# A conv and attention layer in fp32: written order for the convolution's output stage, the norm's rows sooner, and h in x's place

## The chip, the cores and the metric

The kernel runs on one core of a Trainium2 chip. The metric is the device time of one execution in microseconds. The kernel before was timed three times: 1240.5, 1238.94 and 1238.16, a median of 1238.94 us.

Six instruction streams work side by side and meet only at semaphores: PE (TensorE, matrix products), DVE (VectorE), ACT (ScalarE, which also evaluates functions from tables), POOL (GpSimd), SP (SyncE, which issues most of the transfers) and the DMA engines.

## The reference, cut to what matters

One decoder layer over 1024 positions and 1024 channels, with a convolution branch and an attention branch.

```python
mod = c @ w_ada + b_ada
shift, scale, gate = split(mod, 3)
h = _rmsnorm(x, norm_g) * (1.0 + scale) + shift
glu_a, glu_b, z_conv, q, k, v, z_att, g_conv, g_att = split(h @ w_in)

u = glu_a * sigmoid(glu_b)
u = causal_depthwise_conv(u, conv_w, 31 taps) + conv_b
u = silu(_layernorm(u, conv_ln_g, conv_ln_b))
y_conv = (u * silu(z_conv)) @ w_conv_out

att = dilated_window_attention(rope(q, positions), rope(k, positions), v)   # three groups of heads
y_att = (att * silu(z_att)) @ w_att_out
merged = sigmoid(g_conv) * y_conv + sigmoid(g_att) * y_att
return _rmsnorm(x + gate * (merged @ w_o), final_g)
```

The change touches four things in it: how `h` is kept, the layer norm over channels of `u`, the product with `w_conv_out`, and the tables of sines and cosines from `positions`.

## The kernel before

**Layout.** Activations lie with channels in the 128 partitions, eight tiles of 128x1024 for 1024 channels (tile index `kt` or `ct`). A product in fp32 is made from three products of split values: `hh` and `hl` are the high and low part of `h`, `whi` and `wlo` those of a weight, `uh` and `ul` those of the convolution's result `u`. A helper `mm3` (L72 to L75) issues high times high, high times low and low times high, each a matmul of 512 columns. ACT makes high parts by a copy, DVE or POOL makes low parts by a subtraction. A weight arrives as a raw tile `wraw` (128x1024, three of them in turn, loaded by SP at L62).

**Start stage.** `scaled(kt)` (L351) multiplies x by the row of reciprocal norms into `xr` on DVE, and ACT writes it twice with scale and shift (L356): to `hh`, and in full precision to a tile `h`, of which there are two in turn (tag `h32`). SP stores `h` to the scratch `hscr` (L357), and DVE subtracts to get `hl` (L387). The PE loop around L387 takes one tile a turn, 18 matmuls each: three weights, two halves, three products. `shift(kt)` is a weighted sum on DVE over a row of `w_ada` (L169). Later the scratch is read back as `traw` (L512, L515) for the Strassen products, whose sums and differences DVE makes (L525 to L528, L538).

**The hand-written order.** From there to the norm an order by steps holds. A list `groups` has one entry for a group of twelve matmuls. At step n the loop issues what is due: early work, then the group of that step, then evictions and high parts on ACT, low parts on POOL, DVE work, and last the loads; `at(step, rank, fn)` books such work. A `Form` books a weight half's high part three steps ahead of its group and the low part two steps ahead; its tiles `whi`, `wlo` are handed out in turn from three pairs of 128x1024, in halves. A `Raw` books a load. Generators in the list `behind` are DVE work without a due step (the convolution's taps, the norm): `pump` takes pieces from them as a step's budget allows.

**The norm.** When the last convolution is summed, `norm_mean` (L785) makes the row of means on PE (`pm`), `norm_squares` subtracts it (L795) and sums squares on ACT and DVE (L798 to L803). `sums` books the column sums on PE (L128) two steps on; `scales` makes the reciprocal root a step later: ACT's Sqrt with its table load (L112), small operations on DVE (L113 to L117), and the row `lrow` on PE (L818). `norm_apply` (from L828) goes over the eight tiles `vt` of u: times `lrow` on DVE (L834), silu in two halves into PSUM (L837), times `sz` = silu(z_conv) on DVE (L848), high part `uh` on ACT (L851), low part `ul` on POOL (L852). Meanwhile PE runs the last products of the values; ACT copies their results out as `gs` (L633) and SP stores them to `vscr` (L634).

**The output stage.** Behind the loop stand, in program order: the tables from `positions` as one block on DVE (L969 to L988) with two sines on ACT (L983); then the product with `w_conv_out`. Units `d` = 0 to 7 are output tiles of 128 channels. Units 0 and 1 run side by side over the eight tiles of u, 96 matmuls; the other units run one after the other with `project`. Weights come through `weights` (L57 high on ACT, L58 low on DVE, 1024 wide). A unit's result is multiplied by the gate `sgc` on DVE (L1001) and stored (L1002); `modulation` makes a column of `gate_c` from a row of `w_ada` and the broadcast `cb` of c (L169). Attention follows.

## Time and profile before

| quantity | before |
|---|---|
| median of three runs | 1238.94 us (1238.16 to 1240.5) |
| profiled execution | 1237.25 us |
| its span, first to last instruction | 1235.5 us |
| mean granted TensorE clock | 0.986 |
| moved by DMA | 194.49 MB, mean 157 GB/s |

Busy shares and waits follow with the prediction. A timeline row reads: start in us, duration in us, engine, source line, operation, output <- inputs, shape, count, and in brackets the idle time ahead of it with what released it. A wait row reads: the waiting engine, line and tile <- the releaser, then the total, the number of times and the longest. A window row has its stretch, its length, and for each of PE, PE's weight loads, DVE, ACT and POOL the busy time with the number of instructions, then the granted clock, the share of DMA engines busy and GB/s. A DMA row gives the source line's tiles, the count, the size and the median us from issue to landing.

### The profile page before, as it was taken

To read this page: it belongs to the slowest core of one execution; us is meant where nothing else is said; L and a number is where in the kernel's file an instruction comes from. 1 tells how busy PE (TensorE), PEld (TensorE's weight loads), DVE (VectorE), ACT (ScalarE), POOL (GpSimd) and SP (SyncE) were. 2 spreads that over 40 slices of the span, in tenths; PEclk is the share of its full clock that TensorE was granted. 3 is DMA by queue.
4 is the path that set the end of the run, shared out by engine and by line. 5 is a ranking of instruction groups with operands and counts; after the bars stand their busy time and mean duration, and the time that the engine had idled before them with its cause. 6 is when DMAs were issued, how large, how long until landed. Compare 5 with 4: busy or idle time off the path is not lost.

```text
span 1235.5 us, 17342 instructions
## 1 busy us (share of the span) xinstructions
PE 1195.6 (97%) x6042; PEld 1000.4 (81%) x6042; DVE 910.8 (74%) x1500; ACT 585.8 (47%) x1205; POOL 404.1 (33%) x304
## 2 busy tenths in 40 slices
PE   9989999999999999588999999999999999999997
PEld 7777888888888888466888888888888888888886
DVE  7869999999999998684325657777786762559444
ACT  5645334545445445631015666666666655346111
POOL 0003868787787774430031111111111012200000
PEclk9989999999999999888999999999999999999999
DMA  9574333213324247717825555666665564668231
GB/s 361 194 260 169 120 103 120 97 65 103 113 84 136 71 152 289 276 48 251 195 82 150 137 137 144 160 188 144 159 193 144 141 181 132 207 236 298 86 102 68
DMA packets 100189, 194.49 MB, mean 157 GB/s; under 512 B 29635, under 2 KB 43267, under 8 KB 100102
## 3 DMA queue, kind: packets, MB, share of 16 engines
q1 hardware_dynamic: 83424, 186.77, 49.1%
q10 hardware_dynamic: 16678, 6.61, 1.9%
q8 instruction: 48, 0.79, 0.3%
q14 instruction: 39, 0.32, 0.1%
HBM read 122.25 MB, written 39.62 MB: 131 GB/s over the span
## 4 chain that ended last, share of the span: by engine, by line
PE 81%; DVE 11%; ACT 3%; DMA 3%; issue 1%; POOL 0%; SPq 0%; DVEq 0%; ACTq 0%
PE d L73 20%; PE d L75 20%; PE d L74 20%; DVE acc L566 5%; PE o L1308 4%; PE d L624 4%; PE s L1271 3%; PE t L1287 3%; PE d L1601 2%; PE d L1599 2%; PE d L1600 2%; DMA x<-in_xT 1%; DMA wraw<-in_w_v 1%; DVE wa L169 1%; ACT d L837 1%
## 5 line engine op out<-in xcount | busy, mean ns | idle before, releaser
L566 DVE SCALAR_TENSOR_TENSOR acc<-u,cw,acc 128x1024 f32<-128x1024 f32 x232 | 298.8, 1288 | 6.6
L74 PE MATMUL d<-hl,whi 128*128 128x512 f32 x752 | 294.5, 392 | 4.1 <-DVE hl L387 4.1
L73 PE MATMUL d<-hh,whi 128*128 128x512 f32 x752 | 295.8, 393 | 1.2 <-ACT gs L897 0.7
L75 PE MATMUL d<-hh,wlo 128*128 128x512 f32 x752 | 294.4, 391 | 0.5 <-POOL wlo L458 0.5
L58 POOL TENSOR_TENSOR wlo<-wraw,whi 128x512 fp32r<-128x512 f32 (+1 forms) x56 | 81.7, 1476 | 458.5 <-ACT whi L57 433.4
L458 POOL TENSOR_TENSOR wlo<-wraw,whi 128x512 fp32r<-128x512 f32 x114 | 151.7, 1338 | 183.6 <-ACT whi L455 173.3
L75 PEld LDWEIGHTS d<-hh,wlo 128*128 128x128 f32 x752 | 141.8, 189 | 31.3 <-POOL wlo L458 0.9
L74 PEld LDWEIGHTS d<-hl,whi 128*128 128x128 f32 x752 | 141.8, 189 | 30.5 <-DVE hl L387 4.5
L73 PEld LDWEIGHTS d<-hh,whi 128*128 128x128 f32 x752 | 141.8, 189 | 28.5 <-ACT gs L897 1.2
L1280 ACT ACTIVATE sb<-sb,stats 128x128 f32<-128x128 f32 (+1 forms) x192 | 84.8, 443 | 31.7 <-DVE stats L1276 31.4
L1276 DVE CUSTOM_DVE_ANT_0 sb<-s,mask 128x128 f32<-128x128 f32 (+1 forms) x192 | 59.7, 349 | 52.1 <-PE s L1271 50.8
L455 ACT ACTIVATE whi<-wraw 128x512 fp32r<-128x512 f32 x114 | 69.6, 625 | 42.8 <-POOL wraw L728 22.5
L57 ACT ACTIVATE whi<-wraw 128x512 fp32r<-128x512 f32 (+1 forms) x71 | 48.9, 718 | 78.6 <-PE d L74 66.5
L73 PE MATMUL d<-uh,whi 128*128 128x512 f32 x128 | 52.9, 413 | 22.3 <-DVE vt L848 12.7
L1287 PE MATMUL t<-ident,sb 128*128 128x128 f32 x280 | 73.7, 276 | 0.1
L1308 PE MATMUL o<-ph,vt 128*64 128x128 f32 (+1 forms) x432 | 65.9, 253 | 0.0
L1102 ACT ACTIVATE ph<-t 128x384 fp32r<-128x384 f32 (+2 forms) x96 | 45.7, 476 | 38.9 <-PE t L1287 25.8
L1105 DVE TENSOR_TENSOR pl<-t,ph 128x384 fp32r<-128x384 f32 (+2 forms) x96 | 52.0, 542 | 11.4 <-ACT ph L1102 10.8
L1271 PE MATMUL s<-k,ql 128*128 128x128 f32 (+1 forms) x192 | 55.0, 292 | 0.0
L1308 PE MATMUL o<-pl,vt 128*64 128x128 f32 (+1 forms) x216 | 52.8, 261 | 0.0
L74 PE MATMUL d<-ul,whi 128*128 128x512 f32 x128 | 51.9, 405 | 0.0
L1601 PE MATMUL d<-oh,hl 128*128 128x512 f32 (+1 forms) x136 | 51.2, 376 | 0.0
(295 smaller groups left out, 2631.5 us busy)
## 6 DMA issues: line engine op xcount, KB each, us to landing
wraw<-in_w_t SPq DMA_DIRECT2D x67, 512.0 KB, 4.1
k<-kqp SPq DMA_DIRECT2D x96, 128.0 KB, 2.3
q<-kqp SPq DMA_DIRECT2D x96, 128.0 KB, 2.3
wraw<-in_w_v SPq DMA_DIRECT2D x19, 512.0 KB, 4.4
wa<-in_w_ada SPq DMA_DIRECT2D x16, 512.0 KB, 4.8
ql<-kqp SPq DMA_DIRECT2D x48, 128.0 KB, 2.3
wg<-wscr SPq DMA_DIRECT2D x48, 128.0 KB, 3.2
hscr<-h SPq DMA_DIRECT2D x8, 512.0 KB, 2.6
```

Of the source, the lines that this page charges most:

```text
L58: (lo_eng or nc.vector).tensor_sub(lo, raw, hi.bitcast(F32))
L73: nc.tensor.matmul(ps, lh, rh, start=start, stop=False, skip_group_check=again)
L74: nc.tensor.matmul(ps, lh, rl, start=False, stop=False, skip_group_check=again)
L75: nc.tensor.matmul(ps, ll, rh, start=False, stop=stop, skip_group_check=again)
L455: nc.scalar.activation(self.hi, src(), AF.Copy)
L458: nc.gpsimd.tensor_sub(self.lo, src(), self.hi.bitcast(F32))
L566: nc.vector.scalar_tensor_tensor(acc, u[:, k:k + S], cw[:, ct, k:k + 1], acc, op0=mult, op1=add)
L1271: products.append((w, lambda c=c, w=w, l=x[:, ts_], r=k[:, ks], i=i: nc.tensor.matmul(ps[:, c:c + w], l, r, start=i == 0, stop=i == 1)))
L1280: nc.scalar.activation(sb[:, c:c + w], sb[:, c:c + w], AF.Exp, bias=stats[:, t, h, 1:2], scale=-1.0, accum_out=stats[:, t, h, 0:1])
L1287: yield from ((lambda c=c: nc.tensor.transpose(ps[:, c:c + P], sb[:, c:c + P], ident)) for c in range(0, o, P))
L1308: nc.tensor.matmul(out_, l, r, **kw))
L1601: nc.tensor.matmul(ps, hl[:, k, c], rh, start=False, stop=k == KT - 1)
```

## The change

1. `scaled` writes the full-precision `h` back into x's own tile; the two `h32` tiles go (one is left for another use).
2. Scratch space for half tiles becomes whole slots `n3`, `s1`, `sd0`, `sd1`, handed out by halves; the second set of `traw` is loaded two steps later and handled in whole tiles, its high and low parts one step later.
3. The norm's mean is due one step sooner, its column sums one step sooner after the squares, and its scales in the same step as the sums. `norm_apply` holds two PSUM banks for the silus instead of two for each tile, and issues the products of a tile ahead of the next tile's multiply by `lrow`.
4. The tables become a generator `tables` behind the norm.
5. The output stage is part of the list of groups: `first_outputs` makes eight groups, one for each tile of u, with units 0 and 1 side by side; `output` makes four groups for each further unit. Their weights come through `Raw` and `Form`; `Gated` loads the gate and the row of `w_ada` (into a raw tile) two steps ahead of its unit and does the sums in place. `cb` is loaded into the slot of the last `vt` tile.

```diff
-            return st.tile([P, S], F32, name="vs", tag="h32", bufs=2)
+            return st.tile([P, S], F32, name="vs", tag="h32", bufs=1)
...
         def scaled(kt):
             xr = st.tile([P, S], F32, name="xr", tag="xr", bufs=2)
-            h32 = h_of[kt] = st.tile([P, S], F32, name="h32", tag="h32", bufs=2)
+            h32 = h_of[kt] = x_t[kt]
             nc.vector.tensor_mul(xr, x_t[kt], rrow)
             for dst in (hh[:, kt], h32):
                 nc.scalar.activation(dst, xr, AF.Identity, bias=scol[:, kt:kt + 1], scale=gcol[:, kt:kt + 1])
...
-    for x in ("n2", "n3", "n4", "h3", "l3"):
+    for x in ("n2", "n4", "h3", "l3"):
         slot(x, "t")
-    piece("t", "s1", 2), piece("t", "side", 3), piece("t", "gs", 4), piece("t", "pad", 1)
-    for n in range(16):
-        slot(f"t{n}", "t")
+    piece("t", "gs", 4)
+    for x in ("n3", "s1", "sd0", "sd1", *(f"t{n}" for n in range(16))):
+        slot(x, "t")
...
-        return [[t[k] if type(t) is list else t[:, k] for t in tiles] for k in range(2)]
+            tag = ({1: "t1", 3: "t3", 2: "t5", 4: "t8"}, {1: "sd0", 3: "sd1", 2: "s1", 4: "n3"})[c][i]
+            raw = t_raw[i, c] = slot(tag, "traw").rearrange("p (k s) -> p k s", k=2)
+            nc.sync.dma_start(raw, hscr[k0 + 2 * c:k0 + 2 * c + 2, :, wide(half)].rearrange("k p s -> p k s"))
...
-            at(now[0] + 3, EARLY, norm_mean)
+            at(now[0] + 2, EARLY, norm_mean)
...
         def s1():
-            box["s1"] = piece("s1", "s1", 2)
+            box["s1"] = half_piece(("s1",))
...
         def copy(key, src, scale=1.0, sbuf=True):
             def fn():
-                box[key] = piece("side", "side", 3) if sbuf else bank()
+                box[key] = half_piece(("sd0", "sd1")) if sbuf else bank()
                 nc.scalar.activation(box[key], box[src], AF.Copy, scale=scale)
...
         def sums():
             pc = bank()[:, 0:8]
             col_sums(pc, tot2)
-            at(now[0] + 1, POST_, lambda: scales(pc))
-        at(now[0] + 2, EARLY, sums)
+            at(now[0], POST_, lambda: scales(pc))
+        at(now[0] + 1, EARLY, sums)
...
     def norm_apply(lrow):
         for ct in range(4):
             sz_load(ct)
-        sg = {}
+        sg = [bank() for _ in range(2)]
 
         def scaled_(ct):
             nc.vector.tensor_mul(vt[ct], vt[ct], lrow)
-            sg[ct] = [bank() for _ in range(2)]
             for half in range(2):
-                nc.scalar.activation(sg[ct][half], vt[ct][:, wide(half)], AF.Silu, scale=cvec[:, 1, ct:ct + 1],
+                nc.scalar.activation(sg[half], vt[ct][:, wide(half)], AF.Silu, scale=cvec[:, 1, ct:ct + 1],
                                      bias=cvec[:, 2, ct:ct + 1])
 
         scaled_(0)
         yield TAP
         for ct in range(KT):
+            for half in range(2):
+                s = wide(half)
+                nc.vector.tensor_mul(vt[ct][:, s], sg[half], sz_t[ct][:, s])
+            yield 2 * POST
+            hi, lo = slot(f"t{8 + ct}", f"uh{ct}", F32R), slot(f"t{ct - 1}" if ct else "n2", f"ul{ct}", F32R)
+            nc.scalar.activation(hi, vt[ct], AF.Copy)
             if ct + 1 < KT:
                 scaled_(ct + 1)
                 yield TAP
-            for half in range(2):
-                s = wide(half)
-                nc.vector.tensor_mul(vt[ct][:, s], sg[ct][half], sz_t[ct][:, s])
-            yield 2 * POST
-            hi, lo = slot(f"t{8 + ct}", f"uh{ct}", F32R), slot(f"t{ct - 1}" if ct else "n2", f"ul{ct}", F32R)
-            nc.scalar.activation(hi, vt[ct], AF.Copy)
             nc.gpsimd.tensor_sub(lo, vt[ct], hi.bitcast(F32))
             ch[ct], cl[ct] = hi, lo
             if ct + 4 < KT:
                 sz_load(ct + 4)
+        u_ctx.close()
+        tabs.append(c_ctx.enter_context(sbuf_pool("tabs", side="right")))
+        behind.append(tables())
...
+    def tables():
+        ctab, stab = (tabs[0].tile([P, S], F32, name=x) for x in ("ctab", "stab"))
+        tabs.extend((ctab, stab))
+        posi = pb.tile([P, S], I32, name="posi", tag="s1")
+        nc.sync.dma_start(posi, a["positions"].to_broadcast([P, S]))
+        yield GROUP
+        n_ = slot("sd0", "n_")
+        nc.vector.tensor_copy(n_, posi)
+        nc.vector.tensor_scalar(stab, n_, fr[:, 0:1], None, op0=mult)
...
+        for c in (C1, C2, C3):
+            nc.vector.scalar_tensor_tensor(stab, n_, -c, stab, op0=mult, op1=add)
+            yield TAP
...
+        def wrapped_sin(tab, n_):
+            nc.vector.tensor_scalar(n_, tab, PI_IN, -TWO_PI, op0=ALU.is_gt, op1=mult)
+            nc.vector.tensor_add(tab, tab, n_)
+            yield POST + TAP
...
+            yield POST
+            at(now[0] + 1, EVICT, lambda: nc.scalar.activation(tab, n_, AF.Sin))
+
+        nc.vector.tensor_scalar(ctab, stab, TWO_PI / 4, None, op0=add)
+        yield POST
+        yield from wrapped_sin(ctab, n_)
+        yield from wrapped_sin(stab, slot("sd1", "m_"))
+        at(now[0] + 2, POST_, lambda: nc.vector.tensor_scalar(stab, stab, fr[:, 1:2], None, op0=mult))
+
+    cb_of = []
+
+    def cb_load():
+        cb_of.append(slot("t7", "cb"))
+        nc.sync.dma_start(cb_of[0], a["c"].to_broadcast([P, D]))
+
...
+    class Gated:
+
+
+        def __init__(self, step, d):
+            self.d = d
+            at(step - 2, LOAD, self.load)
+
+        def load(self):
+            self.sg = slot(f"n{3 + self.d % 2}", "sgc")
+            nc.sync.dma_start(self.sg, gcscr[self.d])
+            self.wa = load_raw(a["w_ada"][2 * KT + self.d])
+
+        def out(self, half, ps):
+            y = piece("gs", "gs", 4)
+            nc.vector.tensor_mul(y, ps, self.sg[:, wide(half)])
+            spend(POST)
+            nc.sync.dma_start(cscr[self.d][:, wide(half)], y)
+            if half:
+                modulation(2 * KT + self.d, gate_c[:, self.d:self.d + 1], self.wa, self.wa, cb_of[0])
+                spend(TAP)
+
+    def u_block(kh, half):
+        s = wide(half)
+        return lambda k: (ch[4 * kh + k][:, s], cl[4 * kh + k][:, s])
+
+    def first_outputs(step):
+        raws = [Raw(step - 7 + d, a["w_co"][d]) for d in range(2)]
+        forms = {(d, kh): Form(step - 3 + 2 * kh + d, raws[d].half(kh)) for kh in range(2) for d in range(2)}
+        out = [Gated(step + 6 + d, d) for d in range(2)]
+        ps = {}
+
+        def group(k):
+            def fn():
+                for d in range(2):
+                    f = forms[d, k // 4]
+                    c = slice(k % 4 * P, k % 4 * P + P)
+                    for half in range(2):
+                        if k == 0:
+                            ps[d, half] = bank()
+                        mm3(ps[d, half], f.hi[:, c], f.lo[:, c], ch[k][:, wide(half)], cl[k][:, wide(half)],
+                            k == 0, k == KT - 1)
+                if k == KT - 1:
+                    for d in range(2):
+                        for half in range(2):
+                            at(now[0], POST_, lambda d=d, half=half: out[d].out(half, ps[d, half]))
+            return fn
+        return [group(k) for k in range(KT)]
...
+    def output(step, d):
+        raw = Raw(step - 6, a["w_co"][d])
+        forms = [Form(step + 2 * i, raw.half(i)) for i in range(2)]
+        out = Gated(step, d)
...
+        def group(i, half):
+            def fn():
+                if i == 0:
+                    ps[half] = bank()
+                block(ps[half], forms[i], u_block(i, half), i == 0, i == 1)
+                if i:
+                    at(now[0], POST_, lambda: out.out(half, ps[half]))
+            return fn
+        return [group(i, half) for i in range(2) for half in range(2)]
...
+    at(len(groups), LOAD, cb_load)
+    take(first_outputs(len(groups)))
+    for d in range(2, KT):
+        take(output(len(groups), d))
 
     at(-1, HIGH, t_first)
-    at(-1, LOAD, lambda: t_loads(1))
-    at(1, POST_, t_second)
+    at(1, LOAD, lambda: t_loads(1))
...
-    stab = tabs.tile([P, S], F32, name="stab")
-    posi = pb.tile([P, S], I32, name="posi", tag="h3")
-    nc.sync.dma_start(posi, a["positions"].to_broadcast([P, S]))
...
-    cb = slot("h3", "cb")
-
-    def co_load(d):
-        sg_ = slot(f"n{3 + d % 2}", "sgc")
-        nc.sync.dma_start(sg_, gcscr[d])
-        return weights(a["w_co"][d]), sg_
...
-    def gated(d, sg_, wa):
-        def consume(half, s, ps):
-            y = pb.tile([P, 512], F32, name="gs", tag="gs", bufs=4)
-            nc.vector.tensor_mul(y, ps, sg_[:, s])
-            nc.sync.dma_start(cscr[d][:, s], y)
-            if not half:
-                modulation(2 * KT + d, gate_c[:, d:d + 1], wa, slot("l3", "jk"), cb)
-        return consume
...
-    nc.sync.dma_start(cb, a["c"].to_broadcast([P, D]))
-    pair = [co_load(d) for d in range(2)]
-    ps = [bank() for _ in range(4)]
-    for k in range(KT):
-        c = slice(k * P, (k + 1) * P)
-        for i, ((hi, lo), _) in enumerate(pair):
-            for half in range(2):
-                s = wide(half)
-                mm3(ps[2 * i + half], hi[:, c], lo[:, c], ch[k][:, s], cl[k][:, s], k == 0, k == KT - 1)
...
-    ahead = co_load(2)
-    for d in range(2, KT):
-        w, sg_ = ahead
-        if d + 1 < KT:
-            ahead = co_load(d + 1)
-        project(w, gated(d, sg_, wada(d)), KT, lambda k, s: ch[k][:, s], lambda k, s: cl[k][:, s])
+
+    ctab, stab = tabs[1:]
```

The first place is ACT around the norm's reciprocal root. `vt_…` and `uh_…` with a number are single tiles of u, `d` is a PSUM bank, `ACT_TABLE_LOAD` loads a function table. Before:

```order
L455 ACTIVATE whi<-wraw 128x512 x3
L57 ACTIVATE whi<-wraw 128x1024
L112 ACT_TABLE_LOAD
L112 ACTIVATE ltmp<-lcols 128x8
L837 ACT_TABLE_LOAD
L837 ACTIVATE d<-vt_3768,cvec 128x512 x2
L837 ACTIVATE d<-vt_3770,cvec 128x512 x2
L851 ACTIVATE uh_4099<-vt_3768 128x1024
L57 ACTIVATE whi<-wraw 128x1024
```

And in the changed kernel:

```order
L455 ACTIVATE whi<-wraw 128x512 x3
L112 ACT_TABLE_LOAD
L112 ACTIVATE ltmp<-lcols 128x8
L455 ACTIVATE whi<-wraw 128x512 x2
L826 ACT_TABLE_LOAD
L826 ACTIVATE d<-vt_3697,cvec 128x512 x2
L837 ACTIVATE uh_3993<-vt_3697 128x1024
L826 ACTIVATE d<-vt_3699,cvec 128x512 x2
L455 ACTIVATE whi<-wraw 128x512 x2
L837 ACTIVATE uh_4022<-vt_3699 128x1024
```

The last of the three `whi` ahead of the Sqrt is now a half of the first output weight, two more halves stand between Sqrt and Silu, and each `uh` stands ahead of the next tile's silus instead of behind them.

The second place is SP's queue from the output weights on. Before:

```order
L62 DMA wraw<-in_w_ada 128x1024 x2
L967 DMA posi<-in_positions 128x1024
L1010 DMA cb<-in_c 128x1024
L826 DMA sz<-szscr_100 128x1024
L634 DMA vscr<-gs 128x512 x4
L826 DMA sz<-szscr_101 128x1024
L826 DMA sz<-szscr_102 128x1024
L826 DMA sz<-szscr_103 128x1024
L62 DMA wraw<-in_w_co 128x1024
L995 DMA sgc<-gcscr 128x1024 x2
L62 DMA wraw<-in_w_co 128x1024
```

And in the changed kernel:

```order
L615 DMA vscr<-gs 128x512 x4
L892 DMA cb<-in_c 128x1024
L856 DMA posi<-in_positions 128x1024
L62 DMA wraw<-in_w_co 128x1024
L903 DMA sgc<-gcscr 128x1024
L62 DMA wraw<-in_w_ada 128x1024
L903 DMA sgc<-gcscr 128x1024
L62 DMA wraw<-in_w_ada 128x1024
L903 DMA sgc<-gcscr 128x1024
L62 DMA wraw<-in_w_ada 128x1024
L62 DMA wraw<-in_w_co 128x1024
```

`cb` and `posi` moved behind the values' stores, the third `w_co` stands right behind them, and three rows of `w_ada` stand between it and the fourth.

The third place is DVE behind the norm's last product, in the changed kernel; before, all rows of the tables stood in one block there, ahead of the first `gs`:

```order
L868 SCALAR_TENSOR_TENSOR stab<-n__4203,stab 128x1024 x3
L882 TENSOR_SCALAR ctab<-stab 128x1024
L872 TENSOR_SCALAR n__4203<-ctab 128x1024
L873 TENSOR_TENSOR ctab<-ctab,n__4203 128x1024
L908 TENSOR_TENSOR gs<-d,sgc 128x512 x2
L169 ISA wraw,gate_c<-wraw,cb 128x1024
L169 ISA gate_c 128x1
L172 TENSOR_TENSOR gate_c<-gate_c,bada 128x1
L908 TENSOR_TENSOR gs<-d,sgc 128x512 x2
L169 ISA wraw,gate_c<-wraw,cb 128x1024
```

The gating and sums of units 0 and 1 now stand between pieces of the tables; nine more rows of the tables follow behind them and among those of units 2 and 3.

More of the change, by code (lines that the diff above doesn't have):

```diff
@@ L958, in layer @@
             step += 1
-    u_ctx.close()
-    c_ctx = ExitStack()
-    tabs = c_ctx.enter_context(sbuf_pool("tabs", side="right"))
-    ctab = tabs.tile([P, S], F32, name="ctab")
-    stab = tabs.tile([P, S], F32, name="stab")
-    posi = pb.tile([P, S], I32, name="posi", tag="h3")
-    nc.sync.dma_start(posi, a["positions"].to_broadcast([P, S]))
-    n_ = slot("l3", "n_")
-    nc.vector.tensor_copy(n_, posi)
-    nc.vector.tensor_scalar(stab, n_, fr[:, 0:1], None, op0=mult)
-    nc.vector.tensor_scalar(n_, stab, 1.0 / TWO_PI, None, op0=mult)
```

80 lines of the change are left out of this document (30 added, 50 removed).

## The prediction

> **What bounds the kernel now.** I read the page's busy shares and slices first, then the waits of TensorE (PE), then windows and timelines around the long ones.
>
> ```profile
> PE 1195.6 (97%) x6042; PEld 1000.4 (81%) x6042; DVE 910.8 (74%) x1500; ACT 585.8 (47%) x1205; POOL 404.1 (33%) x304
> PE   9989999999999999588999999999999999999997
> PEclk9989999999999999888999999999999999999999
> PE d L73 <- DVE vt L848: 12.7, 1, 12.7
> PE d L73 <- ACT whi L57: 9.6, 2, 5.4
> PE d L74 <- DVE hl L387: 4.1, 1, 4.1
> PE d L143 <- ACT rrow L144: 1.4, 1, 1.4
> PE d L73 <- DVE u L689: 0.5, 1, 0.5
> 130.00:475.00 345.00, 344.53 (x1519) 284.71 (x1518) 329.90 (x288) 153.08 (x260) 266.23 (x205) 1.00 0.34 112
> 512.50:566.00 53.50, 31.22 (x112) 24.38 (x112) 45.41 (x52) 23.51 (x30) 19.69 (x8) 0.78 0.41 142
> ```
>
> PE is busy 97% of the span, so the time is PE's work plus what PE waits. The wait rows (total, times, longest) name two places: 4.1 us for `hl` early on, and 12.7 + 9.6 = 22.3 us around the convolution's output stage, slices 17 to 19. From 130 to 475 us PE is busy 344.53 of 345 us (first number of the row): nothing the change does there can be worth much. A second loss hides inside busy time: in 512.5 to 566 the clock column says 0.78.
>
> ```profile
> 67.61 0.39 PE L73 MATMUL d<-hh,whi 128*128 128x512 f32 x1
> 72.06 0.80 PE L74 MATMUL d<-hl,whi 128*128 128x512 f32 x1 [4.07 <-DVE hl L387]
> ...
> 74.79 0.63 PE L74 MATMUL d<-hl,whi 128*128 128x512 f32 x1
> 75.22 0.63 PE L75 MATMUL d<-hh,wlo 128*128 128x512 f32 x1
> ...
> 555.53 0.80 PE L73 MATMUL d<-uh,whi 128*128 128x512 f32 x1 [5.36 <-ACT whi L57]
> ...
> 561.82 0.80 PE L73 MATMUL d<-uh,whi 128*128 128x512 f32 x1 [4.22 <-ACT whi L57]
> ```
>
> A warm matmul of 512 columns costs 344.53/1519 = 0.227 us (a group of 12 costs 2.72). After the 4.07 us wait the spacing is 0.43 us (74.79 to 75.22): 0.2 us more each. This holds from 72.06 to 77.3, some 13 matmuls, so 2.6 us in all are paid after such a wait; the rows at 555.53 and 561.82, with their 0.80 us, begin the same. Behind the 1.4 us wait (`rrow`) stand no slow matmuls.
>
> So the region 512.5 to 566 loses 53.5 − 112 × 0.227 = **28.1 us**: 22.3 of waits, 5.8 of slow clock. The early place loses 4.07 + 2.6 = **6.7 us**.
>
> **Part A, h in x's place.** ACT's write of `h` waited 5.69 us for the store of an older `h` from one of two tiles; behind it stood `hl`, behind that PE:
>
> ```profile
> 66.60 2.89 DMA hscr<-h
> 69.51 1.24 ACT L356 ACTIVATE h<-xr,scol,gcol 128x1024 f32<-128x1024 f32 x1 [5.69 <-DMA hscr<-h]
> 74.40 1.23 DVE L387 TENSOR_TENSOR hl<-h,hh 128x1024 fp32r<-128x1024 f32 x1
> 78.02 1.22 DVE L387 TENSOR_TENSOR hl<-h,hh 128x1024 fp32r<-128x1024 f32 x1
> ```
>
> With eight x tiles as targets no write waits for a store. `h` of the third tile then runs right behind its `hh` near 63.8 us, `hl` follows on DVE by about 66.3, and PE needs it at 67.8. What is late next is DVE, one `hl` each 78.02 − 74.40 = 3.62 us; PE spends 18 × 0.227 = 4.09 us on a tile, so DVE keeps ahead. Of the 6.7 us I keep **6.0**: the stage behind hangs on the last stores to `hscr`, the raw loads and DVE's chain to `u`, for which PE already waits 0.5 us; it moves up by the stall of 5.69 at most. If the stage follows only in part, 2 remain; at best 6.7.
>
> The larger halves (4 wide operations where 8 half ones were) and slots in place of pieces lie in 105 to 475 us, beside the busy PE: 0, at most 1 either way.
>
> **Part B, norm sooner.** The rows before:
>
> ```profile
> 475.53 1.72 PE pm L785 x4
> 499.05 1.68 PE d L128 x16
> 506.34 0.87 PE lrow L818 x8
> 499.14 1.06 ACT L57 ACTIVATE whi<-wraw 128x1024 fp32r<-128x1024 f32 x1 [3.23 <-PE d L624]
> 500.21 1.28 ACT L112 ACT_TABLE_LOAD   x1
> 493.25 0.33 SPq L62 DMA_DIRECT2D wraw<-in_w_co  x1
> wraw<-in_w_co SPq DMA_DIRECT2D x2, 512.0 KB, 8.3
> 556.48 4.14 DMA wraw<-in_w_co
> ```
>
> The mean `pm` moves up one group of PE, to 472.8. From it to the sums passed 499.05 − 475.53 = 23.5 us; one group less leaves 20.8. With the sums (1.7) and one group (2.7) instead of two behind them, `lrow` would stand at 498.0 without waits, 8.3 us sooner than now. But ACT, in its order, must first make the high half of the first output weight, and that waits for its load. The load follows the low half that frees a raw tile, work that the change doesn't move much; I put its issue at 492.6, just ahead of the old 493.25, and the landing 4.14 us later (the row of an undisturbed load; beside other loads 8.3 was seen). Then 0.53 for the half (of the 1.06 for a whole), 1.28 for the Sqrt table and some 1.6 for the root and five small DVE operations: `lrow` at about 500.3. **New wait 2.3** (1.5 to 6.5).
>
> From here T is the start of `lrow`. The products of the norm:
>
> ```profile
> 514.78 1.47 ACT L837 ACTIVATE d<-vt,cvec 128x512 f32<-128x512 f32 x2
> 516.19 2.02 ACT L633 ACTIVATE gs<-d 128x512 f32<-128x512 f32 x4
> 513.06 1.28 DVE L848 TENSOR_TENSOR vt<-d,sz 128x512 f32<-128x512 f32 x2
> 519.28 17.81 POOL L852 TENSOR_TENSOR ul<-vt,uh 128x1024 fp32r<-128x1024 f32 x7 [2.92 <-DVE wlo L58]
> ```
>
> ACT's next weight half takes a tile that PE still reads, so it waits for T + 0.9 + 2.7; with 0.53 and the Silu table (1.28) the first silu starts at T + 5.6. POOL's first `ul` now stands ahead of a value weight's low half, which PE needs three groups on: a wait of about 3.4 us inside this stage. Per tile of u the chain is two silus (1.4), the second product (0.6), the next multiply by `lrow` (1.2, as another DVE operation of that width at 543.63 below) and hand-overs: 3.4 us, since one pair of banks serves all. The values' last four copies `gs` stand behind the fifth silu: T + 5.6 + 4 × 3.4 + 1.4 = T + 20.6, the first copy ends at T + 21.2, and its bank is the first output group's. Unbroken, that group would start 0.9 + 5 × 2.72 = 14.5 us behind T. **Loss 6.7**, the 3.4 included. The eight interleaved groups then cost 21.8 us, to T + 43.0, and `ul` keeps ahead of them: eight at 17.81/7 = 2.54 with weight halves between end near T + 36.6, before the last group's start at T + 40.2.
>
> **Part C, units two to seven by schedule.** The load of `cb` waits for the last `ul` (its slot), and in SP's queue `posi` and the third weight stand behind it. From T + 36.6, with 4.14 for a load and 0.4 for each issue, `posi` lands near T + 41.1 and the weight near T + 41.6; its half ends some 0.2 behind PE's T + 43.0: **0.2 lost**. The tables now run in pieces on DVE:
>
> ```profile
> 537.67 0.69 DVE L973 TENSOR_SCALAR n__4217<-n__4217 128x1024 f32<-128x1024 f32 x1
> 538.40 3.74 DVE L975 SCALAR_TENSOR_TENSOR stab<-n__4217,stab 128x1024 f32<-128x1024 f32 x3
> 543.63 1.23 DVE L979 TENSOR_TENSOR ctab<-ctab,n__4217 128x1024 f32<-128x1024 f32 x1
> 555.23 1.22 DVE L169 CUSTOM_DVE_ANT_0 jk<-wraw,cb 128x1024 f32<-128x1024 f32 x1
> 569.53 0.69 DVE L1001 TENSOR_TENSOR gs<-d,sgc 128x512 f32<-128x512 f32 x1 [6.50 <-PE d L75]
> ```
>
> `posi` lands near T + 41.1. The eleven operations up to the first wrap, 3.74 + 1.23 + 7 × 0.69 = 9.8 us and up to 2 more beside POOL's work, stand ahead of the first unit's gating (two of 0.69) and its sum with `cb` (1.22), which frees the raw tile for the fourth weight's load. That load is issued at 41.1 + 11.5 + 1.4 + 1.2 and hand-overs, T + 55.4, lands at T + 59.6, and its high half ends at T + 60.2; PE would be there near T + 53.8. **Loss 6.5, then 2.6 of slow clock, and 0.5** for the low half. From then on a unit lasts 48 × 0.227 = 10.9 us, and its loop (load 4.1, high 0.5, wait for POOL's low, 0.5 and 1.3, and hand-overs) 7.6 at most: no further wait.
>
> Sum of the region: 2.3 + 6.7 + 0.2 + 6.5 + 2.6 + 0.5 = 18.8 us lost where 28.1 were: **9.3 gained**. The profiled execution took 1237.25 us: 1237.25 − 6.0 − 9.3 = 1222.0. The median of the runs, 1238.94, is 1.7 above it, so I say **1222**.
>
> **The Trainium skill on the clock.** The rows: waits of 4.07, 4.22 and 5.36 us were followed by slow matmuls, one of 1.4 was not. The page "TensorE: Matmul & The Clock Gate", Part 1, says that an idle window of about 3.4 us halves the clock, that the window is free-running, and that about as long a busy time restores it. By that rule 3.4 us is just the edge, and the trace agrees on both its sides.
>
> **Rivals.**
> - *Slow clock after the new waits too.* Two new waits (3.4, and 6.7 − 3.4 = 3.3 before the first output group) lie between 1.4 and 4.07. If both slow the clock, the first 2.6 us vanish in the wait behind, the second are paid: 1225. The Trainium skill's page "TensorE: Matmul & The Clock Gate" allows it, if its window falls so.
> - *The fourth weight isn't late.* If the tables' first pieces pass DVE before `gs` is due, or the sum with `cb` comes sooner, 6.5 + 2.6 us go: about 1213. Against it: `posi` behind `cb` behind the last `ul`.
> - *Loads land late.* With 8.3 us where I took 4.14, `lrow` loses 4.1 more and the fourth weight 4.1: 1230.
> - *The early gain stays in part:* 2 instead of 6.0: 1226. For it: the 0.5 us wait for `u`.
> - *Slower.* In units two to seven each weight's load waits for an earlier tile's sum or low half and is issued only a unit ahead. If the loop of 7.6 us (with 4.14 for the load) exceeds PE's 10.9 in each of five units, every one waits, and a wait over 4 us adds 2.6. Waits begin from a landing of 4.14 + 3.3 = 7.4 us; the kernel is slower than before from about 11.3, where five waits of 3.9 us take back the gain, and at 11.5, with slow clock behind each, loses 5 × (4.1 + 2.6) = 33: 1255. Against it: loads of 4.1; for it: the 8.3 row, two loads of one stretch.
> - *It doesn't do what it says:* the loss of 28.1 stays, 1231 with part A alone. The order of the engines' rows rules it out.
>
> **How the numbers follow.** Forecast 1222 (1219 to 1224) 0.40; slow clock too (1225) 0.14; early gain partial (1226) 0.08; fourth weight in time (1213) 0.17; loads late (1230) 0.14; slower (1255) 0.07. A measurement tells about 0.2% (2.5 us) from no change. The range leaves out the slower case and the tail of the two outer ones: **1212 to 1231**. Faster by over 0.2% 0.90, same 0.03, slower 0.07.
>
> **What would show it.** Right: no wait for `hl` and clock 1.00 at 72 to 77; `lrow` near 494 (six us of part A included) with a wait of 2 to 3 us ahead of it; a wait of some 3 us for a value weight's low half and one ahead of the first output group; one wait of 6 us for `whi` at the fourth unit, none later. Wrong: `hl` still awaited; waits for `whi` in more than one of units three to seven; a first output group that follows the values unbroken.

## The result, and the profile after

| kernel | median, us | runs | ratio to before (95% interval) |
|---|---|---|---|
| before | 1239.72 | 1238.16 to 1242.87 | 1 |
| changed | 1226.26 | 1226.02 to 1227.28 | 0.989 (0.9869 to 0.9911) |

The change gains 1.1%, 13.5 us by the medians (a fourth run of the kernel before, 1242.87, has joined the three known earlier). The profiled executions are 1237.25 and 1226.17 us, the spans 1235.5 and 1224.4: 11.1 us, where the prediction had 15.3. The direction and the range of 1212 to 1231 held; the forecast of 1222 was 4.3 us too fast, and its own band of 1219 to 1224 was missed. The rest of this document is about where those 4 us are. Where it says third or fourth unit, `d` = 2 or 3 is meant.

The page and the waits of PE in the changed kernel:

```profile
PE 1197.1 (98%) x6042; PEld 1000.4 (82%) x6042; DVE 901.6 (74%) x1488; ACT 587.2 (48%) x1209; POOL 425.1 (35%) x316
PE   9999999999999999898999999999999999999997
PEclk9999999999999999998999999999999999999999
PE d L73 <- ACT whi L455: 6.1, 2, 5.6
PE d L605 <- POOL wlo L458: 3.9, 2, 3.4
PE d L73 <- ACT gs L998: 1.3, 1, 1.3
...
PE d L75 <- POOL wlo L458: 1.1, 1, 1.1
PE d L73 <- DVE u L670: 1.1, 1, 1.1
PE lrow L808 <- DVE lcols L117: 1.1, 1, 1.1
PE d L73 <- ACT gs L614: 0.9, 1, 0.9
```

The dent in slices 17 to 19 has shrunk, the early one is gone, and the clock row has one dented slice instead of four. The three waits of before (12.7, 9.6 and 4.1 us) no longer exist. In their place stand a wait of 3.4 us for a low half, one of 5.6 us for a weight's high half, and small ones.

To place them, the timeline of PE in the changed kernel, with the first matmul behind each wait, the mean `pm`, and the first score of attention:

```profile
466.74 1.88 PE L775 MATMUL pm<-tot,ones 128*128 128x512 f32 x4
...
488.31 1.95 PE L128 MATMUL d<-ones,tot 128*128 128x1 f32 x16 [0.60 <-DVE tot L793]
...
494.17 1.06 PE L808 MATMUL lrow<-ident,lcols 128*128 128x128 f32 x8 [1.07 <-DVE lcols L117]
...
507.05 0.80 PE L605 MATMUL d<-wlo,hh 128*128 128x512 f32 x1 [3.39 <-POOL wlo L458]
...
515.58 0.50 PE L73 MATMUL d<-uh,whi 128*128 128x512 f32 x1 [0.92 <-ACT gs L614]
...
538.17 0.50 PE L73 MATMUL d<-uh,whi 128*128 128x512 f32 x1 [0.49 <-ACT whi L455]
...
540.04 0.50 PE L75 MATMUL d<-uh,wlo 128*128 128x512 f32 x1 [1.13 <-POOL wlo L458]
...
558.01 0.80 PE L73 MATMUL d<-uh,whi 128*128 128x512 f32 x1 [5.61 <-ACT whi L455]
...
648.96 0.22 PE L1308 MATMUL s<-k,q 128*128 128x128 f32 x1
```

The same two marks in the kernel before:

```profile
475.37 1.88 PE L785 MATMUL pm<-tot,ones 128*128 128x512 f32 x4
...
660.68 0.22 PE L1271 MATMUL s<-k,q 128*128 128x128 f32 x1
```

`pm` stands 8.63 us sooner. 2.72 of that is its own move by a group, so the early part gained 5.9 us. The first score stands 11.72 us sooner, so the norm and the output stage gained 11.72 − 5.9 = 5.8 us. The attention stage and the end gave 0.6 back. The prediction had 6.0 and 9.3: of the 4.2 us that are short, 3.5 lie between the norm and attention.

### The profile page after: what moved, and what is told of

It is laid out like the page before. It is cut to its first block, busy times and chain, and to the rows that moved or that the text cites. A ratio compares the mean times of both kernels' runs of the same rounds, so it can differ in the third digit from the quotient of the medians.

```text
span 1224.4 us, 17342 instructions
## 1 busy us (share of the span) xinstructions
PE 1197.1 (98%) x6042; PEld 1000.4 (82%) x6042; DVE 901.6 (74%) x1488; ACT 587.2 (48%) x1209; POOL 425.1 (35%) x316
## 4 chain that ended last, share of the span: by engine, by line
PE 85%; DVE 6%; DMA 3%; ACT 2%; issue 2%; POOL 1%; SPq 0%; ACTq 0%; DVEq 0%; POOLq 0%
PE d L75 20%; PE d L73 20%; PE d L74 20%; PE d L605 4%; PE o L1345 4%; PE d L274 3%; PE s L1308 3%; PE t L1324 3%; PE d L1637 2%; PE d L1636 2%; PE d L1638 2%; DMA wraw<-in_w_co 1%; DVE tot L790 1%; ACT d L826 1%; DVE vt L824 0%
## 5 line engine op out<-in xcount | busy, mean ns | idle before, releaser
L458 POOL TENSOR_TENSOR wlo<-wraw,whi 128x512 fp32r<-128x512 f32 x130 | 173.8, 1345 | 235.4 <-ACT whi L455 235.2
L455 ACT ACTIVATE whi<-wraw 128x512 fp32r<-128x512 f32 x130 | 79.2, 624 | 120.0 <-DMA wraw<-in_w_co 58.4
L605 PE MATMUL d<-wlo,hh 128*128 128x512 f32 x128 | 50.7, 396 | 3.9 <-POOL wlo L458 3.9
L75 PE MATMUL d<-uh,wlo 128*128 128x512 f32 x128 | 51.8, 404 | 1.3 <-POOL wlo L458 1.1
```

The costliest lines, as they stand in the source:

```text
L75: nc.tensor.matmul(ps, ll, rh, start=False, stop=stop, skip_group_check=again)
L455: nc.scalar.activation(self.hi, src(), AF.Copy)
L458: nc.gpsimd.tensor_sub(self.lo, src(), self.hi.bitcast(F32))
L605: nc.tensor.matmul(ps[i], l[:, k, c], r, start=k == 0 and n == 0, stop=k == KT - 1 and n == 2)
```

## The experiments

Twelve runs. Times are medians; before was measured beside each set, at 1238.4 (e1 to e4), 1238.8 (e5 to e8) and 1239.4 us (e9 to e12). Ratios are to before unless another kernel is named.

### Part A alone, and the change without it

```diff
-            h32 = h_of[kt] = st.tile([P, S], F32, name="h32", tag="h32", bufs=2)
+            h32 = h_of[kt] = x_t[kt]
```

e1 makes this edit (and the number of tiles for `vs`) in the kernel before.

> The kernel before with one edit: h is written into x's tile. Theory (the stall at hl was the whole cost of the two h tiles): the 4.07 us wait and the 2.6 us of slow clock go, some 0.8 comes back as waits for gs and u in the stage behind: 6 us less than before, about 1233.5. Rival (the chain from the stores to u takes the gain back unless the second set of raw loads is moved too, as the whole change does): 2 us less, about 1237.5.

Measured: 1234.34 us, ratio 0.9973 (0.9957 to 0.9989), so 1.4 to 5.3 us less (expected 6, rival 2). e9 undoes the same edit in the changed kernel.

> The changed kernel with part A undone: h goes to one of two tiles of its own again. Theory (part A is worth about 6 us, the mean's row pm having come 5.9 us sooner net of its own move): the 4 us wait for hl and its slow clock return: 6 us more than the changed kernel, about 1232. Rival (part A alone gained 4 us, and the later second set of raw loads gives the rest): 4 us more, about 1230.

Measured: 1233.2 us, ratio 0.995 (0.9935 to 0.9966), against 0.989 for the whole change: some 7 us by the medians (3.8 to 8.6 between single runs). In e1 `pm` came 5.26 us sooner, in e9 7.30 us later than in the changed kernel. In e1:

```profile
PE d L143 <- ACT rrow L144: 1.6, 1, 1.6
...
PE d L73 <- DVE u L689: 1.1, 1, 1.1
PE d L73 <- ACT gs L897: 1.1, 1, 1.1
```

The wait for `hl` and its slow clock are gone in e1, and the waits for `u` and `gs` behind grew from 0.5 and 0.7 us to 1.1 each: the 6.7 us lose about 1.0 there, as the prediction had it (0.7). The two ends, 3 to 4 us on the kernel before and 7 on the changed one, lie on both sides of 6, and their ranges overlap: the times don't show that part A is worth more in the changed kernel. In the profiles the move of `pm` differs by 2.0 us between the two pairs; of that only 0.4 shows in the waits for `gs`, and the rest was not settled.

### The fourth weight: posi, cb, and DVE's order

e2, e3, e5 and e6 go at the 5.6 us wait. e2 loads `posi` a step earlier than `cb`:

```diff
+    at(len(groups) - 1, LOAD, posi_load)
     at(len(groups), LOAD, cb_load)
```

> The changed kernel with the load of posi issued a step ahead of cb, so that it no longer stands behind cb (which waits for the last ul). Theory (the fourth weight is late because posi lands late, the tables' first part holds DVE ahead of the first gating and its sum, and that sum frees the raw tile): the tables' first part is done by about 538 us, the 5.6 us wait and the 2.9 us of slow clock and low half at the fourth unit go, the waits at the third unit stay: 8.5 us less than the changed kernel, about 1217.5. Rival (the fourth weight's load is slow in itself, 6.9 us from issue to landing, and would be late wherever its tile is freed): at most 2 us less.

Measured: 1221.6 us, ratio 0.9862 (0.9847 to 0.9877), 4.7 us less than the changed kernel by the medians: half of what was expected. The load of `posi` was no longer late, and still the first gating was. DVE in e2:

```profile
526.92 0.90 DVE L857 CAST n__4189<-posi 128x1024 f32<-128x1024 int32 x1
527.86 0.75 DVE L858 TENSOR_SCALAR stab<-n__4189,fr 128x1024 f32<-128x1024 f32 x1
528.65 2.77 DVE L860 TENSOR_SCALAR n__4189<-stab 128x1024 f32<-128x1024 f32 x1
...
538.14 2.17 DVE L871 TENSOR_TENSOR ctab<-ctab,n__4189 128x1024 f32<-128x1024 f32 x1
...
543.20 1.28 DVE L912 TENSOR_TENSOR gs<-d,sgc 128x512 f32<-128x512 f32 x2
```

From the cast to the gating pass 16.3 us instead of the 10 to 12 of the prediction: operations beside POOL's `ul` and low halves took 2.77 where 0.69 is usual and 2.17 where 1.23 is, and two more operations of the tables now stood ahead of `gs`. So there are two holds, the load and DVE's order. At the third unit the wait for the high half is gone, and one of 0.95 us for the low half is left: POOL's two low halves took 3.95 us there, beside the tables on DVE, where two took 2.55 in e5 without them.

e3 gives `cb` another slot (`sd1`), which is free early, so that SP's queue isn't blocked by the last `ul`. In this kernel both wraps of the tables share `sd0`, and the second wrap writes it before the cosine reads it, so that the cosine table holds other values.

```diff
-        cb_of.append(slot("t7", "cb"))
+        cb_of.append(slot("sd1", "cb"))
```

> The changed kernel with cb in a slot that is free earlier (sd1; the second wrap of the tables uses sd0 again), so that cb, posi, the third weight and the gates no longer stand in SP's queue behind the last ul. Theory (one blocked load, cb, makes both the third and the fourth weight late and lets five loads share the DMA engines): the waits of 0.49 and 1.13 us and the slow clock at the third unit go as well, 2.9 us, beside the 8.5 of the fourth unit: 11 us less than the changed kernel, about 1215. Rival (ACT's high half for the third unit waits for a tile that PE reads until the last interleaved group): the third unit keeps its waits, 8.5 us less.

Measured: 1219.99 us, ratio 0.9853 (0.9838 to 0.9867). The third unit has no wait at all any more, against the rival (a tile that PE still reads): its wait was the load's. The time is 6.3 us less than the changed kernel's, where 11 was expected. The fourth unit keeps 2.4 us, for the same reason as in e2: its first gating starts at 543.16.

e5 adds to e2 that the tables begin behind the gatings of units 0 and 1:

```diff
-        behind.append(tables())
...
+    at(len(groups) - 1, EVICT, lambda: behind.append(tables()))
```

> The run before this one (posi issued ahead of cb) with the tables' first piece due only behind the gatings and sums of units 0 and 1 on DVE. Theory (DVE's order holds the fourth weight: there the first gating stood behind 16 us of tables, from 526.9 to 543.2 us, though posi had landed): the first gating starts at the end of the interleaved groups, near 538, the sum at 540, the fourth weight's load is issued some 5 us sooner, and its wait of 3.0 with 0.6 for the low half and 1.4 of slow clock goes: 5 us less than that run, about 1216.5. Rival (the load queues in itself, behind the gates and rows issued with it): the wait stays above 2 us, about 1220.

Measured: 1221.56 us, ratio 0.9858 (0.9826 to 0.9889): no gain on e2. The first gating does start early, at 537.93, and the fourth weight has no wait left. But the fifth has. PE and SP in e5:

```profile
562.84 0.50 PE L73 MATMUL d<-uh,whi 128*128 128x512 f32 x1 [2.23 <-ACT whi L455]
564.59 0.80 PE L75 MATMUL d<-uh,wlo 128*128 128x512 f32 x1 [1.02 <-POOL wlo L458]
```

```profile
541.44 13.34 SPq L913 DMA_DIRECT2D cscr<-gs  x5
...
555.86 0.38 SPq L62 DMA_DIRECT2D wraw<-in_w_co  x1
```

The load of the fifth weight stands in SP's queue behind five stores of `gs`. The fifth store waits for the third unit's gating, which stood behind tables on DVE, so the load is issued at 555.86 and its high half runs at 562.15. The hold moved one unit on.

e6 is e5 with `cb` in `sd1` (and the second wrap in `s1`).

> The run with the tables behind the first gatings, and in addition cb in slot sd1 (and the second wrap of the tables in s1), so that SP's queue is not held by the last ul and the third weight lands well ahead. Theory: the third unit starts unbroken too; the 1 to 1.6 us of waits there, with up to 1.7 of slow clock, go: 2 us less, about 1214.5. Rival (ACT's high half for the third unit waits for a tile that PE reads until the interleaved groups end): no difference.

Measured: 1216.92 us, ratio 0.9816 (0.9792 to 0.9841). The third and fourth units start unbroken; at the fifth 0.46 and 1.10 us of waits are left. The three edits together are worth 9.3 us by the medians. That this is near the prediction's terms for part C (0.2 + 6.5 + 2.6 + 0.5 = 9.8) is chance: the third and fourth unit of the changed kernel lose 12.3 us (below), and e6 still loses some 3 at the fifth, where nine slow matmuls follow the two waits.

### The norm: two waits that hide each other

e4 puts the next tile's multiply by `lrow` ahead of this tile's products on DVE.

```diff
         for ct in range(KT):
+            if ct + 1 < KT:
+                times_row(ct + 1)
+                yield TAP
             for half in range(2):
                 s = wide(half)
                 nc.vector.tensor_mul(vt[ct][:, s], sg[half], sz_t[ct][:, s])
```

> The changed kernel with the norm's multiply by lrow of the next tile put ahead of the two products of this tile on DVE. Theory (the loop of 3.37 us per tile goes down to about 2.6, but PE is then held by its earlier wait for a value weight's low half, 3.4 us with 1.4 of slow clock, so only the 0.92 us wait for gs ahead of the first output group goes): 1 us less than the changed kernel, about 1225. Rival (the loop itself holds the output stage): 3 us less, about 1223.

Measured: 1226.86 us, ratio 0.9908 (0.9893 to 0.9922), the same as the changed kernel. The 0.92 us wait for `gs` is gone, but the output stage starts at 515.63 as before, since more of the values' matmuls ran slow, and the wait at the fourth unit is 7.83 us instead of 5.61.

e10 leaves the loop alone and books each `ul` a step later, so that the value weights' low halves stand ahead of the first `ul` on POOL.

```diff
-            nc.gpsimd.tensor_sub(lo, vt[ct], hi.bitcast(F32))
-            ch[ct], cl[ct] = hi, lo
+            ch[ct] = hi
+            at(now[0] + 1, POOLED, lambda ct=ct: low_part(ct))
```

> The changed kernel with one edit: each ul is booked a step later, so that on POOL the value weights' low halves stand ahead of the first ul. Theory (the 3.4 us wait for the low half is absorbed: the copies gs set the start of the output stage whatever PE does before): the wait of 3.4 goes and comes back in the one ahead of the first output group, which grows from 0.9 to about 5.5; its slow clock, 2.3 us, is now paid in the output stage: 2 us more than the changed kernel, about 1228.5. Rival (the wait of 3.4 is a loss of its own): 3 us less, about 1223.

Measured: 1228.61 us, ratio 0.9913 (0.9898 to 0.9928): 2.3 us slower by the medians, the number of the theory, but not all by its path. PE in e10:

```profile
508.46 0.50 PE L605 MATMUL d<-wlo,hh 128*128 128x512 f32 x1 [0.73 <-POOL wlo L458]
...
516.94 0.80 PE L73 MATMUL d<-uh,whi 128*128 128x512 f32 x1 [5.69 <-ACT gs L614]
```

A wait of 3.39 us was taken away, and the one behind it grew from 0.92 to 5.69. The output stage starts 21.4 us behind `lrow` (516.94 − 495.51) as in the changed kernel: this half of the theory is shown, and it is the term "loss 6.7, the 3.4 included" of the prediction. Slow matmuls now follow in the output stage, ten of them from 516.94, some 2 us. But the first score stands only 1.33 us later than in the changed kernel (650.29), and `lrow` itself is 1.34 us later. DVE and POOL in e10:

```profile
493.92 1.24 DVE L116 TENSOR_SCALAR ltmp<-ltmp 128x8 f32<-128x8 f32 x1
```

```profile
493.84 1.29 POOL L458 TENSOR_TENSOR wlo<-wraw,whi 128x512 fp32r<-128x512 f32 x1 [0.77 <-ACT whi L455]
```

An operation on eight columns, on the path to `lrow`, takes 1.24 us instead of 0.17, beside a low half that the edit moved there. The slow matmuls are taken up again further on: the third unit has no wait here, and the fourth, held by its load, begins 64.2 us behind `lrow` against 63.8. Of the 2.7 us between the profiled spans (1227.1 and 1224.4) the other 1.4 lie in attention and behind. So e10 shows that the first wait was contained in the second, but not that the slow clock behind it costs anything there.

e7 joins both edits, on e6.

> The run before this one with two more edits in the norm: the next tile's multiply by lrow ahead of this tile's products on DVE, and each ul booked a step later, behind the value weights' low halves on POOL. Theory (the output stage starts late because of a loop of 3.37 us per tile and of one ul that stands ahead of a low half; each hides the other, and the multiply alone gained nothing): the wait of 3.4 us for the low half with its slow clock goes, the copies gs come 3 us sooner, and now nothing behind takes it back: 3 us less, about 1211.5. Rival (PE is held further on, by ul on POOL, as eight of them at 2.4 us and the low halves need 24 us): 1 us less at most.

Measured: 1219.61 us, ratio 0.9839 (0.9813 to 0.9865), 2.7 us slower than e6 by the medians; the theory falls. Its first score stands at 641.30, 1.4 us later than in e6. The loop went only from 3.37 to 3.19 us a tile, since `uh` stands ahead of the next silus on ACT, and the wait ahead of the output stage is 5.11 us with slow clock behind it, as in e10. The loss on DVE and POOL that e10 showed is in e7 too:

```profile
494.12 1.23 DVE L116 TENSOR_SCALAR ltmp<-ltmp 128x8 f32<-128x8 f32 x1
```

```profile
494.05 1.28 POOL L458 TENSOR_TENSOR wlo<-wraw,whi 128x512 fp32r<-128x512 f32 x1 [0.77 <-ACT whi L455]
```

The operation on eight columns ends when POOL's low half ends that started just ahead of it (495.35 and 495.33). It stands on the path to `lrow`, which comes 28.45 us behind `pm` here (495.71 − 467.26) and 27.78 in e6.

e11 books the first output weights' halves a step later, so that ACT's two table loads stand ahead of them.

```diff
-        forms = {(d, kh): Form(step - 3 + 2 * kh + d, raws[d].half(kh)) for kh in range(2) for d in range(2)}
+        forms = {(d, kh): Form(step - 2 + 2 * kh + d, raws[d].half(kh)) for kh in range(2) for d in range(2)}
```

> The changed kernel with one edit: the first output weights' halves are booked one step later, so that ACT's Sqrt and Silu tables stand ahead of them. Theory: lrow no longer waits for the load (1.1 us), the first silu starts some 3 us sooner, ul and the low half of the value weight too, so the first output group starts 3 us sooner; the last ul, cb behind it, and the third and fourth weights move along: 3 us less than the changed kernel, about 1223. Rival (the loads take it back at the fourth unit): no difference.

Measured: 1224.26 us (1222.62 to 1229.96), ratio 0.9893 (0.9864 to 0.9923): not told apart from the changed kernel, with one run of the four far above the rest. In the profile the output stage starts 1.5 us sooner, at 514.04. The fourth unit's wait grows to 7.75 us, but the unit begins 1.9 us sooner (556.07) and the first score stands 2.5 us sooner (646.47): the gain isn't taken back at the fourth unit, against the rival. Whether the whole kernel gains the 3 us of the theory, these runs don't tell.

e8 is e7 with e11's edit.

> The run before this one with the first output weights' halves booked one step later. Theory (ACT's Sqrt stands behind a half whose load lands late, 1.9 us of wait for lrow, and its Silu table behind a half that waits 4.6 us for a tile): lrow comes 1 to 2 us sooner and the first silu 2 more: 3.5 us less, about 1208. Rival (the last value weights or POOL hold PE then): 1 us less at most.

Measured: 1218.14 us (1215.52 to 1222.5), ratio 0.9819 (0.9787 to 0.9852). That is less than the 3.5 us expected, and not told apart from e7. The output stage starts at 512.79, 3.8 us sooner than in e7, and the first score at 638.37 against 641.30; but the profiled execution was the slowest of the four, with a wait of 3.5 us for `pl` in attention that is 0.5 us or less in every other profile here.

e12 is e8 with the next tile's silus ahead of this tile's `uh`.

```diff
-            nc.scalar.activation(hi, vt[ct], AF.Copy)
             if ct + 1 < KT:
                 silus(ct + 1)
+            nc.scalar.activation(hi, vt[ct], AF.Copy)
```

> The run with all parts (cb's slot, posi first, tables behind the gatings, the multiply by lrow ahead, ul a step later, first output halves a step later), and the next tile's silus ahead of this tile's uh on ACT. Theory (with uh ahead of the silus the loop was 3.2 us per tile, ACT waiting 0.76 us for DVE in each; with the silus ahead ACT has 1.5 + 1.0 without a gap): the loop goes to 2.5 us, gs come 2.7 us sooner, the wait of 4.05 us ahead of the first output group shrinks below 1.5 and its slow clock of 1.2 goes: 4 us less than the best run of all parts, about 1212. Rival (POOL's ul at 2.4 us each with the low halves between now hold the interleaved groups): 1216.

Measured: 1215.55 us (1212.54 to 1217.57), ratio 0.9807 (0.9788 to 0.9827). ACT's loop is 2.9 us a tile, where 2.5 was expected, and the wait ahead of the output stage 2.69 us, with slow clock; the time is near the rival's 1216. It beats the changed kernel (0.989) clearly. Against e6 (0.9816) it is not told apart, so the norm's edits are not shown to add anything.

## Why the prediction was right, and where it was off

- **Part A**: 6.0 forecast, 5.9 by the row `pm`. The wait for `hl` and its slow clock vanished together (the clock from 72 to 77 us is 1.00), and `hl` of the third tile ran from 65.49 us, where 65.1 to 66.3 was meant. The waits for `u` and `gs` took 1 us back.
- **`lrow`**: forecast 2.3 us of new wait, near 494 once part A is taken off. It stands at 494.17 with 0.60 + 1.07 us of waits. The Sqrt behind a weight half that waits for its load is as forecast, but only the 1.07 us belong to it, against the sign of 2 to 3 us; the 0.60 is a wait of the column sums for DVE, which was not in the sum.
- **The start of the output stage**: forecast T + 21.2 with T the start of `lrow`; measured 515.58 − 494.17 = 21.4. The 3.4 us wait for the low half is there (3.39; the prediction doesn't show how it came to 3.4, so the agreement to the tenth proves little), and e10 shows that it is contained in the later wait. That one is 0.92 us and not 3.3, since seven slow matmuls from 507.05 and a wait of 0.49 us fill the place. Of the rival *slow clock after the new waits too* the first half came true, and cost nothing, as it said.
- **The third unit**: this step failed. The prediction said 0.2 us lost, from a landing of 4.14 us, and nothing for the low half or the clock. Measured, from 538.17 to where the fourth unit would have begun (558.01 − 5.61 = 552.40) pass 14.2 us, where 48 matmuls need 10.9: 3.3 us, beside the 0.49 ahead of it. The mis-sized term is the landing. (By the prediction's own numbers the high half would end at T + 41.6 + 0.53 = T + 42.1, ahead of PE's T + 43.0; its 0.2 doesn't follow from them.) SP, DVE and ACT in the changed kernel, then the DMA rows from 529 to 540 us:

```profile
530.44 0.33 SPq L892 DMA_DIRECT2D cb<-in_c  x1
530.84 0.41 SPq L856 DMA_DIRECT2D posi<-in_positions  x1
531.31 0.42 SPq L62 DMA_DIRECT2D wraw<-in_w_co  x1
...
550.36 0.33 SPq L62 DMA_DIRECT2D wraw<-in_w_co  x1
```

```profile
535.92 0.69 DVE L859 CAST n__4203<-posi 128x1024 f32<-128x1024 int32 x1 [9.14 <-DMA posi<-in_positions]
...
547.91 1.28 DVE L908 TENSOR_TENSOR gs<-d,sgc 128x512 f32<-128x512 f32 x2
```

```profile
537.49 1.15 ACT L455 ACTIVATE whi<-wraw 128x512 fp32r<-128x512 f32 x2 [9.61 <-PE d L74]
```

```profile
sgc<-gcscr SPq DMA_DIRECT2D x2, 512.0 KB, 6.9
wraw<-in_w_ada SPq DMA_DIRECT2D x2, 512.0 KB, 7.7
cb<-in_c SPq DMA_DIRECT2D x1, 512.0 KB, 4.0
posi<-in_positions SPq DMA_DIRECT2D x1, 512.0 KB, 5.1
wraw<-in_w_co SPq DMA_DIRECT2D x1, 512.0 KB, 6.1
```

  Seven loads of half a megabyte leave within four microseconds, once the last `ul` lets `cb` go, and they share the engines: the first three land after 4.0, 5.1 and 6.1 us, the gates and rows behind them after 6.9 and 7.7 in the median. The prediction took the row of a load that ran alone. With 6.1 the third weight lands at 537.4, right where its high half starts (537.49). The row of that half names PE as the last to release it, which would be a tile that PE still reads. But in e3 and e6, whose loads leave early, the same half runs at 529.94 and 528.06, amid the interleaved groups, and the unit has no wait: that the late load is the cause is shown. POOL's two low halves took 1.73 and 1.79 us beside the tables on DVE, and slow matmuls followed; this was not in the sum.
- **The fourth unit**: forecast 6.5 + 2.6 + 0.5; measured 5.61, then slow matmuls from 558.60 to 563.80 (some 2.5 us) and 0.35 for the low half. The mechanism held: the sum with `cb` frees the raw tile at T + 56.2 (load at 550.36; forecast T + 55.4). That the size held is luck: the load took 6.9 us to land and not 4.14, and PE came 4.4 us later than T + 53.8, mostly for the loss at the third unit, so that two errors offset each other.
- **Units five to eight**: no wait after 563.80, as forecast, but with less room than the 7.6 of 10.9 us said: the fifth weight's high half ran at 568.10, right from its load. e5 shows the tighter rule: a weight's load stands behind the store of the unit two ahead of it in SP's queue.
- **The rest**: attention and the end are 0.6 us longer (from the first score to the end of the span 575.4 us against 574.8), which was taken as zero. And 1.4 us of the region are in none of these terms.
- **From the sum to the forecast**: the sum gave 1222.0 for the profiled execution, and the prediction said 1222 for the median as well, though it put the median 1.7 us higher. Taken along, the 1.7 would have made it 1223.6.

In sum, 18.8 us of new losses were forecast and 28.1 − 5.8 = 22.3 found, 3.5 more. The third unit alone is 3.3 + 0.5 − 0.2 = 3.6 of that; `lrow` (0.6) and the fourth unit (1.1) came out better than forecast, the rest 1.6 worse. Of the rivals, *loads land late* came true in a form of its own: its loss is not at `lrow` and the fourth weight, where it was placed, but at the third. The measured 1226.26 is also the number of *the early gain stays in part*, which did not happen.

## What to carry to other kernels

One blocked transfer in an in-order queue does two kinds of harm: all behind it are late, and when it goes they go together and share the engines; so a load whose slot frees late belongs behind those whose slots are free (e2, with `posi` ahead of `cb`: 4.7 us), or in another slot (e3: 6.3 us; with DVE's order as well, e6: 9.3). Two waits in one stage hide each other: taking away the first alone gains nothing where another chain sets the end (e10), and slow matmuls that the second had hidden come out behind it (e10, e7). What an operation takes alone is a floor: where a DVE operation meets POOL, or a load meets six others, take the crowded row.

## What the runs showed of the hardware

**The clock falls without a long wait.** In the changed kernel two short waits, 0.49 and 1.13 us within 3 us, were followed by half clock; in e6 it was the column sums, 16 matmuls of one column each over 1.95 us with 0.60 us of wait ahead. Windows of the changed kernel (first two rows) and of e6:

```profile
540.60:543.60 3.00, 3.00 (x9) 2.31 (x8) 2.96 (x2) 0.00 (x0) 1.08 (x1) 0.50 0.25 100
491.20:493.70 2.50, 1.91 (x9) 1.24 (x7) 0.58 (x4) 2.27 (x4) 1.29 (x1) 1.00 0.81 246
```

```profile
491.20:493.70 2.50, 2.50 (x7) 1.98 (x6) 0.56 (x4) 2.29 (x4) 1.28 (x1) 0.50 0.71 257
```

The same sums left the clock at 1.00 in the changed kernel and at 0.50 in e6, with a wait of the same 0.60 us. In e8 waits of 0.68 and 1.02 us at the fifth unit were followed by clock 1.00. So a wait of 1 us can cost 2 us more or nothing, and the length of one wait doesn't decide it. The Trainium skill's page "TensorE: Matmul & The Clock Gate", Part 1, says that a free-running window watches activity, which would make the outcome depend on where the window falls; no run here shows the window itself. The edge of 3.4 us, on whose two sides the prediction saw its trace, does not hold in these runs if it is put to single waits: the 1.13 us above was followed by half clock.

**DVE beside POOL.** Full-width operations that took 0.69 and 1.23 us alone took 2.77 and 2.17 us in e2 while POOL worked. The eight-column one took 1.23 to 1.25 instead of 0.17 in e7, e8, e10 and e12, each time beside a low half on POOL. So the two engines do not meet only at semaphores.
